# Feed-forward gate and up: the high weights take both parts of the tokens in one pass of 512 columns

## The chip, the cores and the metric

The kernel runs on one core of one Trainium2 chip, in one launch. The metric is the device time of that launch in microseconds (us); three runs of the kernel before gave 3330.14, 3331.45 and 3333.46 us, the median is 3331.45 us. Lower is better.

## What is computed

256 tokens of width 1024 go through two stacks of layers. The first stack has two layers and the second four; every layer is a feed-forward block, a mixer, and a second feed-forward block, so there are 12 feed-forward blocks and six mixers. Everything is float32.

```python
def swiglu(x, w_gate, w_up, w_down):          # [256,1024] -> 2816 -> 1024
    return (silu(x @ w_gate) * (x @ w_up)) @ w_down
# first stack, layer 0: mixer recurrent_block; layer 1: forgetting_attention
h = h + 0.5 * rms_norm(swiglu(rms_norm(h, g1), ...), post1)
h = h + rms_norm(mixer(rms_norm(h, g2)), post2)
h = h + 0.5 * rms_norm(swiglu(rms_norm(h, g3), ...), post3)
# second stack, four layers: gdn, short_conv, nsa, gdn; no norm behind a block
h = h + 0.5 * swiglu(rms_norm(h, g1), ...)
h = h + mixer(rms_norm(h, g2))
h = h + 0.5 * swiglu(rms_norm(h, g3), ...)
```

The gdn mixer (gated delta rule, 8 heads, two chunks of 128 tokens) solves a triangular system for every head and chunk before it can apply its state.

## The kernel before

**Products.** A float32 operand is split into a high part, rounded to the TensorE's fast 32-bit type, and a low part, the rest. A product is then three matmuls into the same sum: high by high, high by low, low by high (`mm3`, lines 159 to 164; the page's L162, L163, L164 are these three). Weights come by DMA as float32 (`raw`), ScalarE makes the high part `whi` (L150, or L154 with a gain), VectorE the low part `wlo` (L151, L155). A unit is 1024 columns of both.

**A feed-forward block** (`ffn`, line 228). The 2816 hidden columns are worked in 11 groups of 256, gate and up together: four units of weights per group. Group 0 has the tokens as the stationary operand (`rows_group`, L266): one token tile of 128 after the other, 24 matmuls of 512 columns each, after which the 128x256 result is activated (`act`, L242: ScalarE's Tanh L244, VectorE's L245 and L246) and transposed back on TensorE (`split_T` of `hid`, L174). Groups 1 to 10 have the weights as the stationary operand (`cols_group`, L278): for 8 chunks of the width, 2 halves of the columns, gate and up, an `mm3` with 256 token columns moving, 96 matmuls in all, into two PSUM banks. Between groups stand the 24 matmuls of the down product of the group before (`down_mm`, L249, weights in a pool of their own), 512 columns moving.

**Between blocks.** `residual` (L322) adds the block's output to the token tile `h[t]` and calls `prep(t)` (L194): mean square on ScalarE (`rstd`, L189), a power on GpSimd (L191), the scaling `xn` on VectorE (L208 or L210), eight transposes on TensorE (L174, `xn`), and the split into `xh` (ScalarE, L175) and `xl` (VectorE, L176). Tile 0 goes first, then tile 1; the next block's first matmuls use tile 0 alone.

**gdn** (L748 on). Heads go in four groups of two. For each group `wcols` (L410) projects q, k and v with the weights stationary (48 matmuls of 256 columns each for q, k, v), VectorE convolves them, and `chunk` (L852) runs the triangular solve: five levels of L892 on TensorE, `Y` on ScalarE (L895), L898 on TensorE, L900 and L903 on VectorE; the two chunks of tokens go side by side.

**Order and buffers.** The program is written block by block; a scheduler then puts each engine's instructions into one fixed order, by priority and by when a buffer can be had. An engine works through its order without overtaking. PSUM has eight banks, taken through `bank(tag)`:

```python
def bank(self, tag, name="ps"):                       # L101
    return self.psum.tile([128, 512], F32, name=name, tag=tag, bufs={"acc": 4}.get(tag, 2))
```

So "acc" (sums of down and output products, and some of gdn's) has four banks, "gu" (gate and up, projections) two and "tr" (transposes, parts of the mixers) two.

Of the kernel before, what the change touches and what calls it, by code (L numbers as in the profile page):

```python
# [8 lines left out]
F32 = mybir.dt.float32  # L9
# [20 lines left out]
def level_masks():  # L30
    """[128, 448]: the blocks (even, odd) of size 1 next to the diagonal; then for b = 2, 4, .. 32 the even
    columns of the mask of the blocks (odd, even) of size b"""
    i = np.arange(128)
    out = np.zeros((128, 448), np.int32)
    for l in range(6):
        blk = i >> l
        low = (blk[:, None] == blk[None, :] + 1) & (blk[:, None] % 2 == 1)
        if l == 0:
            out[:, :128] = low.T
        else:  # L40
            out[:, 64 + 64 * l:128 + 64 * l] = low[:, blk % 2 == 0]
# [23 lines left out]
class Core:  # L65
# [35 lines left out]
    def bank(self, tag, name="ps"):  # L101
        return self.psum.tile([128, 512], F32, name=name, tag=tag, bufs={"acc": 4}.get(tag, 2))
# [7 lines left out]
    def rows_to_cols(self, name, *srcs):  # L110
        """srcs: DRAM [n, w] each -> SBUF [w, sum n] with row r in column r."""
# [47 lines left out]
    def mm3(self, out, l, r, start, stop, skip=False):  # L159
        """out += l.T @ r for operands split in (high, low) parts."""  # L160
# [5 lines left out]
    def split_T(self, src, xh, xl):  # L166
        """transpose the 128-column chunks of src [128, *] into xh/xl [128, chunks, 128]"""
# [26 lines left out]
    def prep(self, t):  # L194
        """transposed split of h[t], normalized (times row_gain, where there is one), into self.x; the
        transposes are left to flush"""
# [15 lines left out]
        self.late = lambda: [self.split_T(xs[n], *[a[:, t, 4 * n:4 * n + 4] for a in x]) for n in range(2)]  # L212
# [3 lines left out]
    def flush(self):  # L216
        """the transposes that prep left, after other work for the tensor engine"""
# [4 lines left out]
    def row(self, src):  # L222
        """a DRAM row of 1024 in all partitions"""
# [4 lines left out]
    def ffn(self, gates, up, down, gain, post, after=None, also=None):  # L228
        """gate / up: DRAM [1024, 2816]; down: [2816, 1024]; gain: [128, 8] columns;
        post: None or DRAM row [1024] of the gain after the block; after: None or such a row for the  # L230
        norm that follows; also: None or what to set up on the way"""
# [5 lines left out]
        xh, xl = self.x  # L237
# [28 lines left out]
        def rows_group(j, t, gu):  # L266
            tok = slice(t * 128, t * 128 + 128)
            p = self.bank("gu")
            for k in range(8):
                wh, wl = gu[k // 2]  # L270
                self.mm3(p, (xh[:, t, k], xl[:, t, k]), (wh[:, k % 2], wl[:, k % 2]), k == 0, k == 7)
            hid = act(p)
# [95 lines left out]
    def project_out_turns(self, xs, w, post):  # L368
        """the same with one token tile after the other"""
# [40 lines left out]
    def wcols(self, outs, wv, gain, c0, n, x=None):  # L410
        """outs[i] [n, 256] = (x @ W[:, c0 + i n : c0 + (i + 1) n]).T; wv: DRAM [128, 8, N]"""
# [3 lines left out]
        xh, xl = x or self.x  # L415
# [3 lines left out]
        for i, out in enumerate(outs):  # L419
            c = slice(i * n, i * n + n)  # L420
            for k in range(8):
                wh, wl = us[k // kg]
                self.mm3(out, (wh[:, k % kg, c], wl[:, k % kg, c]), (xh[:, :, k], xl[:, :, k]), k == 0, k == 7)

    def short_conv(self, w_in, conv, w_out):
        """conv: [128, 24] columns (tap * 8 + block)"""
# [3 lines left out]
        with self.tc.tile_pool(name="sc", bufs=2) as sp:  # L430
            yh = self.xt.tile([128, 8, 256], F32R, name="xh")
            yl = self.xt.tile([128, 8, 256], F32R, name="xl")
# [990 lines left out]
```

## Time and profile before

| | |
|---|---|
| three runs | 3330.14, 3331.45, 3333.46 us |
| span of the profiled execution | 3325.6 us |
| what lies around the span (median less span) | 5.9 us |
| TensorE busy | 3266.9 us, 98% |
| VectorE, ScalarE busy | 2163.9 us (65%), 1781.7 us (54%) |
| DMA | 543.94 MB, 52.6% of 16 engines |

The span runs from the first to the last instruction of the one execution that was profiled; that execution's whole time is not listed apart, so the median of the runs stands in for it. A matmul's row shows how long that one takes from its start to its end; neighbours overlap, so what one more of them costs is the distance of starts. "PE" is TensorE, "PEld" its weight loads, "DVE" VectorE, "ACT" ScalarE, "POOL" GpSimd.

### The profile page before, as it was taken

How to read it: one execution, taken by the hardware profiler on the slowest of the kernel's cores; microseconds unless marked ns; L12 is line 12 of the kernel's file. 1: busy time of each engine (PE TensorE's matmuls, PEld its weight loads, DVE VectorE, ACT ScalarE, POOL GpSimd, SP SyncE). 2: the span in 40 equal slices, each digit the busy share in tenths (PEclk: the TensorE clock that was granted, in tenths of full speed). 3: DMA queues.
4: the chain of work that ended last, by engine and by line, in shares of the span. 5: the costliest groups of instructions: out<-in, count | busy, mean ns of one | idle time of the engine just before them, and what ended most of it. 6: DMA issues, size and time to landing. Idle time of an engine off the chain costs nothing.

```text
span 3325.6 us, 57379 instructions
## 1 busy us (share of the span) xinstructions
PE 3266.9 (98%) x22022; PEld 2950.3 (89%) x22022; DVE 2163.9 (65%) x4039; ACT 1781.7 (54%) x3277; POOL 82.1 (2%) x106
## 2 busy tenths in 40 slices
PE   8999999999999999999999999999999999999999
PEld 8988898988798998989999989899767989989898
DVE  7667766664666657776566575665767566577764
ACT  6557655554555544555555455554566555454653
POOL 0000000000000000000000000000100000000000
PEclk9999999998899999999999999999999999999999
DMA  8643665644465663336656466566515656532463
GB/s 265 193 132 120 216 198 169 186 152 129 145 192 160 208 185 109 102 99 206 189 178 198 145 198 195 158 206 188 143 52 164 186 161 205 179 102 86 133 201 109
DMA packets 422043, 543.94 MB, mean 164 GB/s; under 512 B 36232, under 2 KB 369096, under 8 KB 421768
## 3 DMA queue, kind: packets, MB, share of 16 engines
q1 hardware_dynamic: 421768, 540.27, 52.6%
q8 instruction: 173, 2.83, 0.3%
q14 instruction: 102, 0.84, 0.1%
HBM read 539.12 MB, written 1.05 MB: 162 GB/s over the span
## 4 chain that ended last, share of the span: by engine, by line
PE 88%; DVE 6%; ACT 3%; issue 2%; POOL 1%; DMA 1%; POOLq 0%; SPq 0%; ACTq 0%; DVEq 0%
PE ps L164 26%; PE ps L162 26%; PE ps L163 26%; PE ps L174 1%; PE ps L892 1%; PE ps L898 1%; DVE wlo L155 1%; PE ps L1286 1%; DVE wlo L151 1%; POOL ss L191 1%; PE ps L1310 1%; PE ps L725 1%; ACT sq L189 1%; PE ps L554 1%; ACT whi L150 0%
## 5 line engine op out<-in xcount | busy, mean ns | idle before, releaser
L162 PE MATMUL ps<-xh,whi 128*128 128x256 f32 (+1 forms) x4704 | 1335.0, 284 | 6.7 <-ACT v L839 2.7
L164 PE MATMUL ps<-xh,wlo 128*128 128x256 f32 (+1 forms) x4704 | 1333.7, 284 | 0.0
L163 PE MATMUL ps<-xl,whi 128*128 128x256 f32 (+1 forms) x4704 | 1332.8, 283 | 0.0
L155 DVE SCALAR_TENSOR_TENSOR wlo<-raw,gains,whi 128x512 fp32r<-128x512 f32 (+1 forms) x1024 | 717.1, 735 | 470.8 <-ACT whi L154 457.3
L154 ACT ACTIVATE whi<-raw,gains 128x512 fp32r<-128x512 f32 (+1 forms) x1024 | 676.7, 707 | 560.1 <-issue 265.3
L162 PEld LDWEIGHTS ps<-xh,whi 128*128 128x128 f32 (+1 forms) x4704 | 895.6, 190 | 14.1 <-ACT v L839 3.1
L163 PEld LDWEIGHTS ps<-xl,whi 128*128 128x128 f32 (+1 forms) x4704 | 895.9, 190 | 6.0
L164 PEld LDWEIGHTS ps<-xh,wlo 128*128 128x128 f32 (+1 forms) x4704 | 895.3, 190 | 1.2
L151 DVE TENSOR_TENSOR wlo<-raw,whi 128x1024 fp32r<-128x1024 f32 (+4 forms) x473 | 569.6, 1209 | 270.4 <-ACT whi L150 268.0
L150 ACT CAST whi<-raw 128x1024 fp32r<-128x1024 f32 (+4 forms) x473 | 488.9, 1038 | 298.9 <-DMA raw<-in_ffn_w_down 126.0
L162 PE MATMUL ps<-whi,hh 128*128 128x512 f32 x1056 | 412.7, 391 | 0.0
L163 PE MATMUL ps<-wlo,hh 128*128 128x512 f32 x1056 | 412.6, 391 | 0.0
L164 PE MATMUL ps<-whi,hl 128*128 128x512 f32 x1056 | 411.3, 390 | 0.0
L162 PE MATMUL ps<-whi,xh 128*128 128x512 f32 (+3 forms) x624 | 249.2, 400 | 3.0 <-ACT xh L175 3.0
L164 PE MATMUL ps<-whi,xl 128*128 128x512 f32 (+3 forms) x624 | 245.4, 394 | 2.4 <-DVE xl L176 2.4
L163 PE MATMUL ps<-wlo,xh 128*128 128x512 f32 (+3 forms) x624 | 246.0, 394 | 0.0
L164 PEld LDWEIGHTS ps<-whi,hl 128*128 128x128 f32 x1056 | 197.8, 188 | 43.3 <-DVE hl L293 1.8
L162 PEld LDWEIGHTS ps<-whi,hh 128*128 128x128 f32 x1056 | 198.8, 188 | 38.8 <-ACT hh L292 2.0
L163 PEld LDWEIGHTS ps<-wlo,hh 128*128 128x128 f32 x1056 | 198.3, 188 | 37.5
L244 ACT ACTIVATE hid<-ps 128x256 f32<-128x256 f32 x264 | 99.7, 378 | 132.5 <-PE ps L164 132.2
L245 DVE SCALAR_TENSOR_TENSOR hid<-hid,ps 128x256 f32<-128x256 f32 x264 | 110.2, 418 | 74.4 <-ACT hid L244 74.3
L164 PEld LDWEIGHTS ps<-whi,xl 128*128 128x128 f32 (+2 forms) x624 | 116.7, 187 | 28.1 <-DVE xl L176 6.8
(403 smaller groups left out, 2757.2 us busy)
## 6 DMA issues: line engine op xcount, KB each, us to landing
raw<-in_ffn_w_gate_up SPq DMA_DIRECT2D x704, 256.0 KB
raw<-in_ffn_w_down SPq DMA_DIRECT2D x264, 512.0 KB
raw<-in_ffn_w_gate SPq DMA_DIRECT2D x176, 256.0 KB
raw<-in_ffn_w_up SPq DMA_DIRECT2D x176, 256.0 KB
raw<-in_gdn_w_in SPq DMA_DIRECT2D x64, 512.0 KB
raw<-in_sc_w_in SPq DMA_DIRECT2D x24, 512.0 KB
raw<-in_w_kv SPq DMA_DIRECT2D x16, 512.0 KB
raw<-in_gdn_w_out SPq DMA_DIRECT2D x16, 512.0 KB
```

Of the source, the lines that this page charges most:

```text
L150: nc.scalar.copy(hi, raw)
L151: nc.vector.tensor_sub(lo, raw, f32(hi))
L154: nc.scalar.activation(hi[:, i], raw[:, i], AF.Copy, scale=gain[i])
L155: nc.vector.scalar_tensor_tensor(lo[:, i], raw[:, i], gain[i], f32(hi[:, i]), op0=OP.mult, op1=OP.subtract)
L162: mm(out, l[0], r[0], start=start, stop=False, skip_group_check=skip)
L163: mm(out, l[0], r[1], start=False, stop=False, skip_group_check=skip)
L164: mm(out, l[1], r[0], start=False, stop=stop, skip_group_check=skip)
L174: nc.tensor.transpose(p[:, k], src[:, (i + k) * 128:(i + k + 1) * 128], self.ident)
L189: nc.scalar.activation(sq, p, AF.Square, scale=1 / (32.0 * scale), accum_out=ss[:, i:i + 1])
L191: nc.gpsimd.tensor_tensor(ss[:, 3:4], ss[:, 2:3], self.mhalf[:, :1], op=OP.pow)
L244: nc.scalar.activation(hid, p[:, :256], AF.Tanh, scale=0.5)
L245: nc.vector.scalar_tensor_tensor(hid, hid, 1.0, p[:, :256], op0=OP.add, op1=OP.mult)
```

## The change

In groups 1 to 10 the matmul with the high weights takes the high and the low tokens in one pass: 256 columns of the high part and 256 of the low part, side by side, into one whole bank; a second matmul of 256 columns adds low weights by high tokens to the first half of that bank. The two halves are added afterwards (`joined`): ScalarE copies the second half to SBUF, VectorE adds the first. The loop over the two column halves `i` becomes the outer one, with a bank for gate and one for up in each, four in all where there were two. For this, "gu" and "tr" become one tag of four banks, and the high and low tokens become one tile, in which they alternate by chunk. `hid` has two buffers in place of three.

```diff
     def bank(self, tag, name="ps"):
-        return self.psum.tile([128, 512], F32, name=name, tag=tag, bufs={"acc": 4}.get(tag, 2))
+        return self.psum.tile([128, 512], F32, name=name, tag="acc" if tag == "acc" else "gu", bufs=4)
...
     def by_token(self):
-        return [self.xt.tile([128, 8, 256], F32R, name=n).rearrange("p a b -> p (a b)")
-                .rearrange("p (t k c) -> p t k c", t=2, k=8) for n in ("xh", "xl")]
+        return self.xt.tile([128, 4096], F32R, name="x").rearrange("p (t k l c) -> p t k l c", t=2, k=8, l=2)
...
-        def act(p):
-            hid = dpool.tile([128, 256], F32, name="hid", bufs=3)
-            nc.scalar.activation(hid, p[:, :256], AF.Tanh, scale=0.5)
-            nc.vector.scalar_tensor_tensor(hid, hid, 1.0, p[:, :256], op0=OP.add, op1=OP.mult)
-            nc.vector.scalar_tensor_tensor(hid, hid, 0.5, p[:, 256:], op0=OP.mult, op1=OP.mult)
+        def act(g, u):
+            hid = dpool.tile([128, 256], F32, name="hid", bufs=2)
+            nc.scalar.activation(hid, g, AF.Tanh, scale=0.5)
+            nc.vector.scalar_tensor_tensor(hid, hid, 1.0, g, op0=OP.add, op1=OP.mult)
+            nc.vector.scalar_tensor_tensor(hid, hid, 0.5, u, op0=OP.mult, op1=OP.mult)
             return hid
+        def joined(p):
+            o = dpool.tile([128, 256], F32, name="sum", bufs=3)
+            nc.scalar.copy(o, p[:, 256:])
+            nc.vector.tensor_add(o, o, p[:, :256])
+            return o
...
         def cols_group(j, gu):
-            ps = [self.bank("gu") for _ in range(2)]
-            for k in range(8):
-                wh, wl = gu[k // 2]
-                for i in range(2):
+            hs = []
+            for i in range(2):
+                ps = [self.bank("gu") for _ in range(2)]
+                for k in range(8):
+                    wh, wl = gu[k // 2]
                     for half in range(2):
                         cc = slice(256 * half + 128 * i, 256 * half + 128 * i + 128)
-                        self.mm3(ps[i][:, half * 256:half * 256 + 256], (wh[:, k % 2, cc], wl[:, k % 2, cc]),
-                                 (xh[:, :, k], xl[:, :, k]), k == 0 and half == 0, k == 7, True)
-            hs = []
-            for i in range(2):
-                hid = act(ps[i])
+                        nc.tensor.matmul(ps[half], wh[:, k % 2, cc], x[:, :, k].rearrange("p t l c -> p l t c"),
+                                         start=k == 0, stop=False, skip_group_check=True)
+                        nc.tensor.matmul(ps[half][:, :256], wl[:, k % 2, cc], x[:, :, k, 0],
+                                         start=False, stop=k == 7, skip_group_check=True)
+                hid = act(joined(ps[0]), joined(ps[1]))
                 hh = dpool.tile([128, 256], F32R, name="hh", bufs=4)
```

In the new file the two matmuls are L298 and L300, the copy L256 and the add L257; each of L298 and L300 stands 3840 times in the program (12 blocks, 10 groups, 32). Other users of the tokens only follow the new layout.

The change also moves instructions on TensorE, at places that the diff doesn't show. The first is the passage from one feed-forward block to the next in the second stack. `hh`, `hl` are the hidden columns of the block that ends (its down product), `xn` the normalized tokens to transpose, `whi` and `xh` (or `x`) the first products of the block that begins, with token tile 0. Before:

```order
L164 MATMUL ps<-whi,hl 128x512
L162 MATMUL ps<-whi,xh 128x512
L163 MATMUL ps<-wlo,xh 128x512
L164 MATMUL ps<-whi,xl 128x512
...
L174 MATMUL ps<-ident,xn 128x128 x8
L162 MATMUL ps<-whi,xh 128x512
L163 MATMUL ps<-wlo,xh 128x512
...
L174 MATMUL ps<-ident,hid 128x128 x2
L163 MATMUL ps<-wlo,xh 128x512
```

With the change:

```order
L164 MATMUL ps<-whi,hl 128x512
L174 MATMUL ps<-ident,xn 128x128 x8
L162 MATMUL ps<-whi,x 128x512
L163 MATMUL ps<-wlo,x 128x512
L164 MATMUL ps<-whi,x 128x512
...
L174 MATMUL ps<-ident,hid 128x128 x2
L162 MATMUL ps<-whi,x 128x512
```

Fifteen products of tile 0 stood ahead of the transposes of tile 1 and now stand behind them; and the transposes of `hid` stood seven products into tile 1, and now stand ahead of all of them.

The second place is the triangular solve of gdn, at the first group of heads: L892 and L898 (L900 and L906 in the new file) are two steps of a level, and `xh,whi` with 256 columns are the projections of the group of heads that comes next. Before:

```order
L892 MATMUL ps<-XX,NA 128x64 x4
L162 MATMUL ps<-xh,whi 128x256
L163 MATMUL ps<-xl,whi 128x256
L898 MATMUL ps<-Y,XX 128x64 x4
L164 MATMUL ps<-xh,wlo 128x256
L162 MATMUL ps<-xh,whi 128x256
L163 MATMUL ps<-xl,whi 128x256
L164 MATMUL ps<-xh,wlo 128x256
L892 MATMUL ps<-XX,NA 128x64 x4
```

With the change:

```order
L880 MATMUL ps<-kb,k 128x128 x2
L882 MATMUL ps<-q,k 128x128 x2
L900 MATMUL ps<-XX,NA 128x64 x2
L906 MATMUL ps<-Y,XX 128x64 x2
L900 MATMUL ps<-XX,NA 128x64 x4
L906 MATMUL ps<-Y,XX 128x64 x4
```

Between the first L872 and the first transpose behind the solve stood 106 products of the next group; now there is none, and they stand behind the solve.

## Rows read from the trace of the kernel before

**Rows 1.** The page: span, busy time of the engines, chain that ended last.
```profile
span 3325.6 us, 57379 instructions
...
PE 3266.9 (98%) x22022; PEld 2950.3 (89%) x22022; DVE 2163.9 (65%) x4039; ACT 1781.7 (54%) x3277; POOL 82.1 (2%) x106
...
PE 88%; DVE 6%; ACT 3%; issue 2%; POOL 1%; DMA 1%; POOLq 0%; SPq 0%; ACTq 0%; DVEq 0%
```
**Rows 2.** Timeline, TensorE, one group: start us, us, engine line operation out<-in shapes.
```profile
369.99 0.28 PE L162 MATMUL ps<-xh,whi 128*128 128x256 f32 x1
...
381.50 0.40 PE L162 MATMUL ps<-whi,hh 128*128 128x512 f32 x1
...
386.97 0.28 PE L162 MATMUL ps<-xh,whi 128*128 128x256 f32 x1
```
**Rows 3.** Windows, that group: stretch, length, busy us (count) per engine, clock, DMA.
```profile
369.99:386.97 16.98, 16.98 (x122) 16.02 (x120) 11.27 (x18) 10.91 (x17) 0.00 (x0) 1.00 0.69 217
```
**Rows 4.** Groups by shape: count | busy us, mean ns of one | idle before.
```profile
L245 DVE SCALAR_TENSOR_TENSOR hid<-hid,ps 128x256 f32<-128x256 f32 x264 | 110.2, 418 | 74.4 <-ACT hid L244 74.3
...
L244 ACT ACTIVATE hid<-ps 128x256 f32<-128x256 f32 x264 | 99.7, 378 | 132.5 <-PE ps L164 132.2
```
**Rows 5.** Timeline, TensorE, from a feed-forward block to the next, second stack.
```profile
1672.82 0.39 PE L164 MATMUL ps<-whi,hl 128*128 128x512 f32 x1
1673.05 0.39 PE L162 MATMUL ps<-whi,xh 128*128 128x512 f32 x1
...
1676.26 0.39 PE L164 MATMUL ps<-whi,xl 128*128 128x512 f32 x1
1677.02 1.07 PE L174 MATMUL ps<-ident,xn 128*128 128x128 f32 x8 [0.37 <-DVE xn L208]
```
**Rows 6.** Timeline, VectorE, the same passage.
```profile
1674.37 1.23 DVE L151 TENSOR_TENSOR wlo<-raw,whi 128x1024 fp32r<-128x1024 f32 x1 [0.43 <-ACT whi L150]
...
1676.38 0.88 DVE L208 TENSOR_SCALAR xn<-h,ss 128x512 f32<-128x512 f32 x2 [0.67 <-POOL ss L191]
```
**Rows 7.** Timeline, TensorE, such a passage in the first stack.
```profile
528.08 0.39 PE L164 MATMUL ps<-whi,hl 128*128 128x512 f32 x1
...
537.21 0.39 PE L164 MATMUL ps<-whi,xl 128*128 128x512 f32 x1
538.46 1.06 PE L174 MATMUL ps<-ident,xn 128*128 128x128 f32 x8 [0.86 <-DVE xn L208]
```
**Rows 8.** Timeline, TensorE, first product of tile 1 and transposes of hid.
```profile
1680.00 0.39 PE L162 MATMUL ps<-whi,xh 128*128 128x512 f32 x1
...
1681.64 0.41 PE L174 MATMUL ps<-ident,hid 128*128 128x128 f32 x2
```
**Rows 9.** Windows, gdn's first three solves, from L872 to the transposes behind.
```profile
1309.92:1340.26 30.34, 30.34 (x260) 29.47 (x259) 24.12 (x65) 16.61 (x48) 0.70 (x1) 1.00 0.28 82
1351.06:1384.82 33.76, 33.76 (x256) 31.23 (x257) 26.24 (x67) 17.53 (x50) 0.70 (x1) 1.00 0.39 110
1402.13:1432.32 30.19, 30.08 (x254) 28.89 (x255) 23.38 (x63) 16.82 (x49) 0.69 (x1) 1.00 0.21 68
```
**Rows 10.** Timeline, one level of the first solve, all engines.
```profile
1321.11 1.00 PE L892 MATMUL ps<-XX,NA 128*128 128x64 f32 x8
...
1321.75 0.27 ACT L895 COPY Y<-ps 128x128 f32<-128x128 f32 x1 [1.91 <-PE ps L892]
...
1322.23 1.00 PE L898 MATMUL ps<-Y,XX 128*128 128x64 f32 x8
...
1322.83 0.75 DVE L900 COPY_PREDICATED XX<-masks,ps 128x128 f32<-128x128 uint8 x2 [0.72 <-PE ps L898]
...
1323.61 0.67 PE L892 MATMUL ps<-XX,NA 128*128 128x64 f32 x5
```
**Rows 11.** Windows, behind the first block's end: clock in the last column but two.
```profile
201.10:204.10 3.00, 1.64 (x10) 0.84 (x8) 1.75 (x5) 1.71 (x5) 2.44 (x5) 1.00 0.00 0
204.10:211.20 7.10, 7.04 (x27) 5.98 (x27) 5.50 (x9) 1.92 (x5) 4.76 (x8) 0.76 0.34 58
```

More of the change, by code (lines that the diff above doesn't have):

```diff
@@ L178, in by_token, with by_chunk @@
     def by_token(self):
-        return [self.xt.tile([128, 8, 256], F32R, name=n).rearrange("p a b -> p (a b)")
-                .rearrange("p (t k c) -> p t k c", t=2, k=8) for n in ("xh", "xl")]
+        return self.xt.tile([128, 4096], F32R, name="x").rearrange("p (t k l c) -> p t k l c", t=2, k=8, l=2)
+    def by_chunk(self):
+        y = self.xt.tile([128, 4096], F32R, name="x").rearrange("p (l k c) -> p l k c", l=2, k=8)
+        return y[:, 0], y[:, 1]
     def rstd(self, parts, scale=1.0):
@@ L211, in prep @@
             xs.append(xn)
-        self.late = lambda: [self.split_T(xs[n], *[a[:, t, 4 * n:4 * n + 4] for a in x]) for n in range(2)]
+        self.late = lambda: [self.split_T(xs[n], *[x[:, t, 4 * n:4 * n + 4, l] for l in range(2)]) for n in range(2)]
         if t == 1:
@@ L236, in ffn @@
         dv = down.rearrange("(k p) n -> p k n", p=128)
-        xh, xl = self.x
+        x = self.x
         acc = [[None, None], [None, None]]
@@ L270, in rows_group @@
                 wh, wl = gu[k // 2]
-                self.mm3(p, (xh[:, t, k], xl[:, t, k]), (wh[:, k % 2], wl[:, k % 2]), k == 0, k == 7)
-            hid = act(p)
+                self.mm3(p, (x[:, t, k, 0], x[:, t, k, 1]), (wh[:, k % 2], wl[:, k % 2]), k == 0, k == 7)
+            hid = act(p[:, :256], p[:, 256:])
             hh = dpool.tile([128, 2, 128], F32R, name="hh", bufs=4)
@@ L414, in wcols @@
         kg = 1024 // w
-        xh, xl = x or self.x
+        x = self.x if x is None else x
         us = [self.weights([(0, wv[:, k0:min(8, k0 + kg), c0:c0 + w])],
@@ L422, in wcols @@
                 wh, wl = us[k // kg]
-                self.mm3(out, (wh[:, k % kg, c], wl[:, k % kg, c]), (xh[:, :, k], xl[:, :, k]), k == 0, k == 7)
+                self.mm3(out, (wh[:, k % kg, c], wl[:, k % kg, c]), (x[:, :, k, 0], x[:, :, k, 1]), k == 0, k == 7)
     def short_conv(self, w_in, conv, w_out):
@@ L430, in short_conv @@
         with self.tc.tile_pool(name="sc", bufs=2) as sp:
-            yh = self.xt.tile([128, 8, 256], F32R, name="xh")
-            yl = self.xt.tile([128, 8, 256], F32R, name="xl")
+            yh, yl = self.by_chunk()
             bT = sp.tile([128, 4, 256], F32, name="bT", bufs=1)
@@ L516, in recurrent @@
         with self.tc.tile_pool(name="rg", bufs=2) as sp:
-            yh = [self.xt.tile([128, 8, 256], F32R, name="xh"), sp.tile([112, 4, 256], F32R, name="yh", bufs=1)]
-            yl = [self.xt.tile([128, 8, 256], F32R, name="xl"), sp.tile([112, 4, 256], F32R, name="yl", bufs=1)]
+            yh, yl = [[a, sp.tile([112, 4, 256], F32R, name=n, bufs=1)] for a, n in zip(self.by_chunk(), ("yh", "yl"))]
             ys = [(yh[c // 8][:112, c % 8], yl[c // 8][:112, c % 8]) for c in range(12)]
@@ L624, in project @@
         kg = min(8, 1024 // w)
-        xh, xl = x or self.x
+        x = self.x if x is None else x
         us = [self.weights([(i * w0, wv[:, k0:k0 + kg, c:c + w0]) for i, c in enumerate(cs)],
@@ L631, in project @@
             p = self.bank(tag)[:, :w]
-            tok = slice(t * 128, t * 128 + 128)
             for k in range(8):
                 wh, wl = us[k // kg]
-                self.mm3(p, (xh[:, t, k], xl[:, t, k]), (wh[:, k % kg], wl[:, k % kg]), k == 0, k == 7)
+                self.mm3(p, (x[:, t, k, 0], x[:, t, k, 1]), (wh[:, k % kg], wl[:, k % kg]), k == 0, k == 7)
             yield t, p
@@ L640, in project_few @@
         nc = self.nc
-        xh, xl = x or self.x
+        x = self.x if x is None else x
         wh, wl = self.weights([(0, wv[:, :, c0:c0 + w])], None if gain is None else [gain[:, k:k + 1] for k in range(8)], (8, w))
@@ L644, in project_few @@
         for k in range(8):
-            self.mm3(p, (wh[:, k], wl[:, k]), (xh[:, :, k], xl[:, :, k]), k == 0, k == 7)
+            self.mm3(p, (wh[:, k], wl[:, k]), (x[:, :, k, 0], x[:, :, k, 1]), k == 0, k == 7)
         y = pool.tile([w, 256], F32, name="few", bufs=1)
@@ L705, in forgetting @@
             qT = sp.tile([128, 8, 256], F32, name="qT", bufs=1)
-            yh = self.xt.tile([128, 8, 256], F32R, name="xh")
-            yl = self.xt.tile([128, 8, 256], F32R, name="xl")
+            yh, yl = self.by_chunk()
             for i in range(0, 8, 2):
@@ L798, in gdn @@
             nc.scalar.activation(eg, gc[:, 1], AF.Exp)
-            yh = self.xt.tile([128, 8, 256], F32R, name="xh")
-            yl = self.xt.tile([128, 8, 256], F32R, name="xl")
+            yh, yl = self.by_chunk()
             def inputs(gr):
@@ L1182, in nsa @@
             vcd = one("vcd", [128, 8, 2, 64])
-            bhl = [self.xt.tile([128, 8, 256], F32R, name=n) for n in ("xh", "xl")]
+            bhl = self.by_chunk()
             def compress(i):
@@ L1245, in nsa @@
             caught_up()
-            yh = self.xt.tile([128, 8, 256], F32R, name="xh")
-            yl = self.xt.tile([128, 8, 256], F32R, name="xl")
+            yh, yl = self.by_chunk()
             pcT = one("pcT", [128, 2, 256])
```

## The prediction

> **What bounds the kernel now.** I read the page first. TensorE is busy for 98% of the span, and 88% of the chain that ended last is its matmuls [rows 1]: an engine that never rests, so a change pays where it takes work from TensorE and costs where it makes TensorE wait. Next the timeline of one feed-forward group, to price a matmul by the distance of starts and not by its row. The 96 matmuls of gate and up start from 369.99 to 381.50, 11.51 us, or 119.9 ns each; the 24 of the down product take from there to 386.97, 5.47 us, or 227.9 ns each [rows 2]. So 512 columns cost less than twice 256: about 12 ns per matmul don't depend on its columns. In the same group VectorE has 11.27 us to do in 16.98 and ScalarE 10.91 [rows 3]: room on both.
>
> That is the inside of a group. Then I looked at the places where the order of TensorE changes, because 98% busy means that the order of before has something to do at every wait. At the passage between blocks the last down product starts at 1672.82, tile 0 of the next block fills the time from 1673.05 to 1676.26, and tile 1's transposes come at 1677.02, when `xn` is ready after an idle 0.37 us [rows 5]. The wait of almost 4 us for the residual, the mean square, the power and the scaling is there today; it is covered. In gdn the solve waits for ScalarE and VectorE at every step and is covered by projections: three stretches of 30 to 34 us with TensorE busy throughout [rows 9].
>
> **The change, part by part.**
>
> *1. One matmul fewer in three.* Three of 256 cost 359.7 ns; one of 512 and one of 256 cost 347.8: 11.9 ns less [rows 2]. The pattern of 512 and 256 by turns is not in the trace; where 512 follows 256 and the other way round (381.50, 386.97) the starts show nothing extra. 3840 times 11.9 ns is **-45.7 us**. At the least it is nothing, at the most the 12 ns of overhead and a little more, 50 us. The Trainium skill (TensorE: Matmul & The Clock Gate, section on the back-to-back issue gap) gives a warm gap of columns divided by 2.4 GHz plus 2.5 ns, which makes 327.5 ns of the three and 325.0 of the two, and a gain of 9.6 us; the measured distances lie 11 and 12 ns above that rule, and the sum goes by them.
>
> *2. Copies and adds.* Per group four copies of 128x256 on ScalarE, priced as its Tanh at 378 ns, and four adds on VectorE at 418 [rows 4]: 10.91 becomes 12.4 and 11.27 becomes 12.9 us of a group that now takes 16.6 [rows 3]. TensorE stays the bound and these cost nothing inside. Behind the last group of a block there is no next group: copy, add, Tanh, two products, cast and difference are some 3 us of such rows, and with the weight splits queued between them about 4.7, against 19 down products that still stand ahead, 4.3 us. I take 0.4 us for each of 12 blocks, **+5 us**, between nothing and 12.
>
> *3. The passages.* The new order puts all transposes of tile 1 ahead of the first product of tile 0, at every passage between a block and a mixer or the next block: 18 of them, counting the start. Transposes and gate/up sums now draw on the same four banks, and TensorE cannot overtake. What covered the wait comes after it. At the passage shown 15 matmuls move behind it, 15 x 228 ns = 3.4 us [rows 5]. By the two orders, there move 24 matmuls at six passages (the first stack and the entry to the second), 18 and 16 at two, 15 at three, 13 at four, 12 at two, 5 at the start: 304, at 228 ns 69 us. One in the first stack, in full: products of tile 0 until 537.21, an idle 0.86 us, transposes at 538.46 [rows 7]; there the wait is longer than its cover, so all 5.5 us are lost. I take off 3 us, because the first product behind the transposes no longer waits for their copies: **+66 us**. The wait itself may shrink, since tile 0's activation and some weight splits now come later: one such split of 1.23 us stands in the way in the passage shown [rows 6]. Up to 0.6 us each, so the lower end is 55; the upper is 69.
>
> *4. Transposes of `hid`.* At 1680.00 tile 1's first product starts, and the transposes of tile 0's `hid` run at 1681.64, seven products later [rows 8]. They now stand ahead of all products of tile 1, and TensorE waits those 1.64 us out: 12 blocks, **+20 us**. For tile 1 the new order has eleven down products in between, 2.5 us: covered, nothing.
>
> *5. gdn.* Each gdn has four solves. By the orders 123, 85 and 118 projections stood inside the first three up to the last transpose behind them; six are left, so 320 x 119.9 ns = 38.4 us leave the cover and come afterwards. Against that an uncovered solve is faster. One level takes 2.50 us [rows 10]; without projections the first `Y` is ready at 1322.02, L898 can follow and L900 after that, and I read 2.0 us off the same rows. Five levels give back 2.5 us, the next group's convolution on VectorE, no longer between the steps, some 2 more: 4.5 in each of three, 13.5. Each group then waits about 1 us more for its own convolution. 38.4 - 13.5 + 3 = 28 us, twice: **+56 us**. Bounds: a solve of 30.34 us holds 106 projections, 12.7 us, so TensorE's own part is 17.6 [rows 9]. If nothing but that were left, a gdn would lose only the waits and the products of the output projection that now stand in one block, some 6 us, 12 for both; if no solve got faster, 41, or 83.
>
> *6. The other mixers* lose cover too (in nsa the compressed blocks' transposes and the rotations, elsewhere less). I count five or six waits of 1 to 3 us: **+10 us**, between 0 and 25.
>
> *7. The clock.* Behind the first block TensorE had little but transposes from 201.10 to 204.10, and in the 7.10 us that follow its granted clock is 0.76 on average [rows 11]: part at 1.2 GHz, the rest at 2.4, a loss of 0.24 x 7.1 = 1.7 us. Waits of that length, covered today, become bare at 18 passages. I take seven such stretches, **+12 us**, between 2 and 31.
>
> **The sum.** -45.7 + 5 + 66 + 20 + 56 + 10 + 12 = +123 us on the span of 3325.6 [rows 1], 3449; with the 5.9 us around it, **3454 us** against a median of 3331.45, 3.7% slower. The gain is real and of its full size, and what moves costs nearly four times as much.
>
> **The rivals.**
>
> *Faster.* The waits shrink when nothing stands beside them. Much of a covered wait may be queueing: VectorE is busy for 24 of the 30 us of a solve [rows 9], largely with the convolution of the next heads, and the same at the passages. If the 18 passages exposed 1 us each in place of 3.7 and the solves fell to TensorE's own 17.6 us: -46 + 5 + 18 + 10 + 4 = -9, 3322 us. It decides once terms 3 to 7 together stay under some 40 us. Against it: in [rows 5] TensorE is idle ahead of the transposes although it had 15 products to do, and in [rows 6] `xn` waits for the power, not for VectorE. 7%.
>
> *Half of it hides.* The solves alone come near TensorE's own time, the passages go as summed: -46 + 5 + 60 + 18 + 16 + 5 + 4 = +62, 3394 us. For it: L892 and L898 show 2.0 us of a 2.5 us level as TensorE's own [rows 10]. 21%.
>
> *The pass gives nothing.* The overhead goes with the columns, so that 512 with a change of weights every time cost twice 256; or its four pieces of 128 columns stream worse than two. Then term 1 falls to 0 to 10 us: 3490 to 3500 us. By the skill's rule above it would be 3490. Against it: the 227.9 ns already hold a change of weights each [rows 2]. 8%.
>
> *More at the low clock.* The long bare waits of the first stack and gdn's bare solves pull the clock down beyond seven stretches, say 30 of them at 1.7 us: +51 in place of +12, about 3493 us. For it: [rows 11] fell after 3 us. Against it: TensorE stays at work in the solves. 12%.
>
> **How the numbers follow.** The forecast, with its terms within a third of what I take, has 49% and covers some 3415 to 3490. With the last two rivals upwards (0.08 + 0.12) and the hidden half downwards (0.21) I reach 3375 to 3545; the lower end is the sum with every term at its low end, -46 + 0 + 55 + 18 + 12 + 0 + 2 = +41, the upper with high ends, -46 + 12 + 69 + 20 + 83 + 25 + 31 = +194, 3525, and a little for both rivals at once. A difference of 0.2% (7 us) is about what a measurement of this kernel can tell from no change. Faster by more: 0.07, the first rival less its part near zero and a little from elsewhere; the same: 0.03; slower: 0.90.
>
> **What would show it.** Right: L298 and L300 start 228 and 120 ns apart inside a group, 32 pairs in 11.1 us; some 4 us (second stack) to 10 us (first stack) without a product between the last down product and tile 0's first; 1.6 us ahead of the transposes of `hid`, in each block; gdn's solves at 25 to 28 us with nothing of `x` between L900 and L906; TensorE's busy share well under 98%. Wrong: pairs at 360 ns (term 1), solves near 18 us (term 5), tile 1's `xn` ready within 2 us of the last down product (term 3), clock rows under 1.00 over tens of us (term 7).

## The result and the profile after

The changed kernel takes **3611.4 us** (median of 4 runs, 3605.5 to 3613.2) where the kernel before took 3331.6 in the same comparison: the ratio is 1.083, with an interval of 1.081 to 1.085. The forecast was slower, 3454 us; the loss is 280 us and not 123, and lies above the range.

The page of the kernel after, with the lines that answer to [rows 1], and the clock in 40 slices of the span:

```profile
span 3608.0 us, 50616 instructions
...
PE 3357.1 (93%) x18182; PEld 2865.1 (79%) x18182; DVE 2343.8 (65%) x4519; ACT 1934.9 (54%) x3759; POOL 83.8 (2%) x106
...
PEclk9999999997999997789999999999899999967999
...
PE 86%; DVE 7%; ACT 3%; issue 2%; POOL 1%; DMA 1%; SPq 0%; POOLq 0%; ACTq 0%; DVEq 0%
```

There are 3840 matmuls fewer, and yet TensorE is busy for 90 us more (3357.1 against 3266.9). Inside a group the change takes time off TensorE (below), so its work elsewhere must take longer, and the line of the clock says why: the mean granted clock is 0.939, where before it was 0.990. A share at 1.2 GHz of 2 x (1 - 0.939) is 440 us of the span; before it was 67. The first seven is the forgetting attention (812 to 902 us), where the kernel before has a low clock too; the other sevens and the six stand in the two gdn stages.

Inside a group the change does what it was forecast to do. The timeline of one group, TensorE, as [rows 2], and its window, as [rows 3]:

```profile
424.24 0.39 PE L298 MATMUL ps<-x,whi 128*128 128x512 f32 x1
...
435.34 0.40 PE L162 MATMUL ps<-whi,hh 128*128 128x512 f32 x1
...
440.83 0.39 PE L298 MATMUL ps<-x,whi 128*128 128x512 f32 x1
```
```profile
424.24:440.83 16.59, 16.59 (x90) 14.21 (x88) 11.64 (x21) 10.01 (x19) 0.00 (x0) 1.00 0.59 187
```

Gate and up run from 424.24 to 435.34: 32 pairs in 11.10 us, 347 ns a pair, forecast 347.8. The group takes 16.59 us in place of 16.98, 0.39 less, 47 us over 120 groups. Copies and adds stand on ScalarE and VectorE beside it, with 10.01 and 11.64 us of 16.59.

At a passage (second stack, and behind it one of the first) the last down product, tile 1's transposes, tile 0's first product and the transposes of `hid` answer to [rows 5], [rows 7] and [rows 8]:

```profile
1813.66 0.39 PE L164 MATMUL ps<-whi,hl 128*128 128x512 f32 x1
1817.85 1.94 PE L174 MATMUL ps<-ident,xn 128*128 128x128 f32 x8 [3.80 <-DVE xn L212]
1819.44 0.78 PE L162 MATMUL ps<-whi,x 128*128 128x512 f32 x1
...
1828.36 0.41 PE L174 MATMUL ps<-ident,hid 128*128 128x128 f32 x2 [1.48 <-DVE hid L250]
```
```profile
545.60 0.39 PE L164 MATMUL ps<-whi,hl 128*128 128x512 f32 x1
547.53 1.06 PE L174 MATMUL ps<-ident,xn 128*128 128x128 f32 x8 [1.54 <-DVE xn L212]
555.90 1.94 PE L174 MATMUL ps<-ident,xn 128*128 128x128 f32 x8 [7.30 <-DVE xn L212]
```

The waits are bare, as forecast: 3.80 us in the second stack, 7.30 in the first, 1.48 ahead of `hid`. New is what follows: eight transposes take 1.94 us where they took 1.07 [rows 5]. They run at half clock, and so do the first eight of tile 0's 24 products (0.43 us apart to 1823.00, 0.23 behind). The windows of the 24 products of tile 0 and of the same 24 of tile 1 right behind:

```profile
1819.44:1826.88 7.44, 7.44 (x26) 5.65 (x24) 1.39 (x2) 0.71 (x2) 0.00 (x0) 0.76 0.25 74
1828.52:1834.07 5.55, 5.55 (x26) 4.60 (x26) 3.55 (x6) 4.21 (x7) 0.00 (x0) 1.00 0.09 18
```

The same work, 7.44 us at a granted clock of 0.76 and 5.55 at 1.00. In gdn it goes further. The windows of the first three solves, as [rows 9] (where they took 30.34, 33.76 and 30.19 us, all at 1.00), and a level of the first, all engines, as [rows 10]:

```profile
1364.80:1400.80 36.00, 31.01 (x154) 29.09 (x152) 16.10 (x51) 9.97 (x36) 0.70 (x1) 0.57 0.09 28
1433.42:1480.62 47.20, 40.63 (x202) 35.66 (x201) 23.36 (x59) 15.18 (x42) 0.70 (x1) 0.71 0.23 66
1512.37:1547.09 34.72, 29.96 (x154) 28.34 (x153) 15.69 (x49) 9.97 (x36) 0.69 (x1) 0.61 0.08 28
```
```profile
1376.48 1.91 PE L900 MATMUL ps<-XX,NA 128*128 128x64 f32 x8
...
1377.63 0.27 ACT L903 COPY Y<-ps 128x128 f32<-128x128 f32 x1 [2.29 <-PE ps L900]
...
1378.18 1.92 PE L906 MATMUL ps<-Y,XX 128*128 128x64 f32 x8
...
1379.89 0.63 PE L900 MATMUL ps<-XX,NA 128*128 128x64 f32 x2
```

The first solve has 154 matmuls in place of 260 and takes 36.0 us in place of 30.3. Its levels show no gap on TensorE at all: eight products of 64 columns take 1.91 us, where before they took 1.00, and a level takes 3.41 us (1376.48 to 1379.89), where before it took 2.50. The solve was to become a chain of waits; at 1.2 GHz it is a chain of TensorE.

Where TensorE waits is shown by the view of waits of the kernel after (engine, line, what it waited for: us in all, times, longest):

```profile
PE ps L174 <- DVE xn L212: 67.8, 22, 8.5
PE ps L174 <- DVE xn L214: 32.5, 12, 6.7
PE ps L174 <- DVE on L980: 23.3, 22, 3.0
PE ps L900 <- DVE XX L894: 22.5, 12, 2.8
PE ps L823 <- ACT th L857: 21.8, 6, 3.6
PE ps L174 <- DVE hid L250: 12.3, 8, 2.0
PE ps L797 <- DVE g L794: 12.1, 2, 6.1
```

In the kernel before, the same view has 23.3 us for `xn` (15.2 and 8.1), and of the other five only `on`, with 1.5 us, among its eleven longest. The four of gdn (`on`, `XX`, `th`, `g`) make 80 us.

### The profile page after: what moved, and what is told of

Same layout as the page of the kernel before. It is cut to its first block, busy times and chain, and to the rows that moved or that the text cites. A ratio compares the mean times of both kernels' runs of the same rounds, so it can differ in the third digit from the quotient of the medians.

```text
span 3608.0 us, 50616 instructions
## 1 busy us (share of the span) xinstructions
PE 3357.1 (93%) x18182; PEld 2865.1 (79%) x18182; DVE 2343.8 (65%) x4519; ACT 1934.9 (54%) x3759; POOL 83.8 (2%) x106
## 4 chain that ended last, share of the span: by engine, by line
PE 86%; DVE 7%; ACT 3%; issue 2%; POOL 1%; DMA 1%; SPq 0%; POOLq 0%; ACTq 0%; DVEq 0%
PE ps L298 24%; PE ps L162 13%; PE ps L163 12%; PE ps L164 12%; PE ps L300 12%; PE ps L174 2%; PE ps L906 1%; PE ps L900 1%; DVE wlo L151 1%; ACT sq L193 1%; POOL ss L195 1%; PE ps L1317 1%; DVE wlo L155 1%; PE ps L1293 1%; PE ps L734 1%
## 5 line engine op out<-in xcount | busy, mean ns | idle before, releaser
L298 PE MATMUL ps<-x,whi 128*128 128x512 f32 x3840 | 1338.9, 394 | 0.0
L300 PE MATMUL ps<-x,wlo 128*128 128x256 f32 x3840 | 1065.0, 277 | 0.0
L298 PEld LDWEIGHTS ps<-x,whi 128*128 128x128 f32 x3840 | 720.1, 188 | 166.2
L300 PEld LDWEIGHTS ps<-x,wlo 128*128 128x128 f32 x3840 | 721.2, 188 | 3.9
L256 ACT COPY sum<-ps 128x256 f32<-128x256 f32 x480 | 169.5, 367 | 396.6 <-PE ps L300 392.5
L257 DVE TENSOR_TENSOR sum<-sum,ps 128x256 f32<-128x256 f32 x480 | 187.7, 417 | 296.6 <-ACT sum L256 296.6
L162 PE MATMUL ps<-whi,x 128*128 128x512 f32 (+3 forms) x624 | 259.5, 416 | 1.0 <-ACT x L175 0.9
L162 PE MATMUL ps<-x,whi 128*128 128x256 f32 (+2 forms) x864 | 259.3, 300 | 0.0
L163 PE MATMUL ps<-x,whi 128*128 128x256 f32 (+2 forms) x864 | 256.0, 296 | 0.0
L164 PE MATMUL ps<-x,wlo 128*128 128x256 f32 (+2 forms) x864 | 255.8, 296 | 0.0
L163 PE MATMUL ps<-wlo,x 128*128 128x512 f32 (+3 forms) x624 | 251.9, 404 | 0.3 <-DVE wlo L155 0.3
L164 PE MATMUL ps<-whi,x 128*128 128x512 f32 (+3 forms) x624 | 250.3, 401 | 0.0
```

The lines of the kernel that those rows point to most:

```text
L162: mm(out, l[0], r[0], start=start, stop=False, skip_group_check=skip)
L163: mm(out, l[0], r[1], start=False, stop=False, skip_group_check=skip)
L164: mm(out, l[1], r[0], start=False, stop=stop, skip_group_check=skip)
L256: nc.scalar.copy(o, p[:, 256:])
L257: nc.vector.tensor_add(o, o, p[:, :256])
L298: nc.tensor.matmul(ps[half], wh[:, k % 2, cc], x[:, :, k].rearrange("p t l c -> p l t c"), start=k == 0, stop=False, skip_group_check=True)
```

## The experiments

All experiments are named by their labels. Two theories stood at the start. A: the line that lets sums and transposes draw on one set of four banks moves TensorE's order, the order makes the loss, and the clock is a large part of it. B: something else in the change (copies, adds, one tile for the tokens) makes it.

### The line on the banks alone, and the change without it

`e1_one_tag` is the kernel before with this line alone:

```diff
-        return self.psum.tile([128, 512], F32, name=name, tag=tag, bufs={"acc": 4}.get(tag, 2))
+        return self.psum.tile([128, 512], F32, name=name, tag="acc" if tag == "acc" else "gu", bufs=4)
```

> The kernel before with one line changed: the sums of gate and up and all transposes draw on one set of four banks (as in the change). Nothing else of the change is in it: three matmuls of 256 columns as before, tokens in two tiles, no copies and adds. Theory A (the shared set of banks alone moves the order, and the order makes the loss): TensorE's order is that of the change at every passage, transposes of hid and in gdn, so the run shows the loss without the gain: the 280 us of the change plus the 50 us that its groups gained (12 blocks x 10 groups x 0.394 us = 47 us), some 3655 us (3635 to 3675), with some 45 stretches at 1.2 GHz as in the change, over 400 us in all. Rival B (the copies and adds of halves, the tokens in one tile or the longer end of a block make the loss): within 60 us of the kernel before, 3331 to 3390 us, with few stretches at 1.2 GHz.

Measured: 3648.1 us, 1.095 of the kernel before (1.093 to 1.096), mean clock 0.940. `e3_turns` is the change with that line undone and with one more:

```diff
-                ps = [self.bank("gu") for _ in range(2)]
+                ps = [self.bank(("gu", "tr")[i]) for _ in range(2)]
```

> The change with two lines altered: banks are in two sets of two again (one for the sums, one for transposes), and the pass of 512 columns takes its two banks from the one set for the first 128 columns of a group and from the other for the second. Gain, copies, adds and the one tile of tokens stay. Theory A (order): TensorE's order in gdn and at the passages is that of the kernel before again; gain of the groups 47 us, copies and adds at the ends of 12 blocks +5 us: 3285 to 3295 us, clock as before (about 70 us at 1.2 GHz). Rival B (the pass itself, its copies and adds or the one tile of tokens make the loss): slower than 3331 us, 3400 to 3600 us.

Measured: **3288.2 us, 0.988 of the kernel before (0.985 to 0.991)**, mean clock 0.990. It beats both kernels: by 45 us the one before (3332.8 in this comparison), by 323 the change. The page of `e3_turns`, then windows of its first solve and of one group:

```profile
span 3285.3 us, 50585 instructions
...
PE 3222.8 (98%) x18182; PEld 2735.6 (83%) x18182; DVE 2322.4 (71%) x4519; ACT 1917.8 (58%) x3757; POOL 83.8 (3%) x106
```
```profile
1294.93:1325.27 30.34, 30.34 (x261) 29.47 (x260) 23.99 (x65) 16.62 (x49) 0.70 (x1) 1.00 0.26 82
371.02:387.61 16.59, 16.59 (x89) 14.22 (x88) 13.46 (x24) 9.70 (x18) 0.00 (x0) 1.00 0.80 248
```

So the loss comes with one line (315 us here, where the change has 323 over `e3_turns`) and goes with it; theory B falls. The group has the 16.59 us of the change, and the solve has the 30.34 us of the kernel before, with 261 matmuls where that had 260. That banks of one set are handed out in the order of the program, and that this keeps later work from being moved ahead, is how I read it; `e4_gdn_only` and `e5_not_gdn` below, which impose that order with two sets, fit it.

`e3_turns` is also the measure of the rest. It runs the same 18182 matmuls as the change, and the difference of the two spans, 322.7 us, splits into 134.3 us that TensorE is busy longer (3357.1 - 3222.8) and 188.4 us that it is idle longer.

`e2_two_tags` undoes the line alone, so that the pass has two banks only.

> The change with the line on the banks alone undone: sums draw on two banks, transposes on two. The pass of 512 columns then has both its banks taken by the first 128 columns of a group, and the second 128 must wait until copy and add have read them. Theory A (banks are what the pass needs; the order is that of the kernel before): a copy of 0.37 and an add of 0.42 us, twice, stand between the halves of a group; where down products lie between them it costs nothing, where not 0.5 to 1 us for each of 120 groups: 3288 to 3400 us, in every case well under the change. Rival (the order moves back only with two more banks for the pass): near the change, 3550 us or more.

Measured: 3341.3 us, 1.002 (1.000 to 1.004). Its view of waits starts with a line that `e3_turns` doesn't have:

```profile
PE ps L298 <- DVE sum L257: 23.9, 24, 2.0
```

The order is back, but the gain is gone: the first product of the pass waits for the add of the half before. The pass needs its second pair of banks, and `e3_turns` takes it where the transposes leave theirs unused.

### gdn and the rest apart

`e4_gdn_only` and `e5_not_gdn` are `e3_turns` with banks taken by turns in the order of the program, in gdn alone or everywhere else; `e0_all` does it everywhere. The lines that all three share:

```diff
+        if self.pooled and tag != "acc":
+            self.turn += 1
+            tag = ("gu", "tr")[self.turn % 2]
...
```

> As e3_turns, but within gdn alone the sums and transposes take the four banks by turns in the order of the program, so that gdn has the order of the change (no projections inside its solves) and the passages and the other mixers have that of the kernel before. Theory A (most of what the forecast missed lies in gdn, where bare solves run at 1.2 GHz): each gdn stage 85 to 100 us longer than in e3_turns, with some 120 us at 1.2 GHz in each: e3_turns + 170 to 200 us, 3455 to 3490 us. By the forecast's own term for gdn: e3_turns + 56 us (12 to 83), 3340 to 3370 us. Rival C (the miss lies in the passages and in the other mixers): under e3_turns + 60 us as well.

Measured: 3454.0 us, 166 over `e3_turns`, mean clock 0.957. The windows of both gdn stages, from the last sum of the block ahead to the first of the block behind, in `e3_turns`, in `e4_gdn_only` and in the change:

```profile
1240.40:1481.11 240.71, 234.17 (x1683) 210.20 (x1681) 182.11 (x454) 125.72 (x302) 18.00 (x20) 1.00 0.35 107
2868.99:3109.80 240.81, 234.23 (x1682) 210.22 (x1681) 182.18 (x454) 125.97 (x302) 18.00 (x20) 1.00 0.35 104
```
```profile
1241.27:1566.49 325.22, 285.14 (x1683) 256.13 (x1681) 187.04 (x454) 129.09 (x302) 16.29 (x20) 0.82 0.26 79
2952.15:3276.41 324.26, 284.60 (x1682) 255.34 (x1681) 187.02 (x454) 129.23 (x302) 16.29 (x20) 0.83 0.26 77
```
```profile
1294.83:1643.31 348.48, 290.50 (x1696) 264.07 (x1694) 191.16 (x459) 131.78 (x305) 16.29 (x20) 0.81 0.25 76
3086.91:3435.29 348.38, 290.55 (x1695) 264.12 (x1694) 190.99 (x459) 131.85 (x305) 16.29 (x20) 0.81 0.25 74
```

The two stages lose 168 us in `e4_gdn_only` and 215 in the change, of a loss of 323. Theory A's range, 170 to 200 us, began 4 us too high; the forecast's own term for gdn, 56 us, is far off.

> The counterpart of e4_gdn_only: gdn keeps the order of the kernel before (two sets of two banks), everything else takes the four banks by turns, in the order of the program, as in the change. If the loss is the sum of its places, this costs what is left of it: 3611 - 3288 - 166 = 157 us over e3_turns, 3445 us (3430 to 3460), of which the forecast's terms for passages, transposes of hid, other mixers and clock make 66 + 20 + 10 + 12 = 108 us. If gdn and the rest share a cost (a clock that falls in one and is paid in the other), the sum of both is off by more than 20 us.

> All stages take the two sets of two banks by turns in the order of the program (gdn as in e4_gdn_only, the rest as in e5_not_gdn). This tells what e4 and e5 leave open: they add 166 and 111 us to e3_turns, together 277, where the change has 323. If the places add and the missing 47 us are those in which taking turns is not the same as one set of four (seven products of tile 1 stand ahead of the transposes of hid, a passage of the first stack differs), this run is at 3288 + 277 = 3565 us (3555 to 3578). If gdn and the rest make each other worse, it is near the change, 3600 us or more.

Measured: `e5_not_gdn` 3398.8 us, 111 over `e3_turns` and not 157; `e0_all` 3535.7 us and not 3565. Both expectations fail, for two reasons. The first is a double count: the passages into and out of gdn were moved in `e4_gdn_only` and in `e5_not_gdn` alike, and the gdn stages of the latter are 27 us longer (253.9 and 254.5 us, from 1278.06 and 2966.86, in place of 240.7 and 240.8). Counted once, 166 + 111 - 27 = 250 us, and `e0_all` has 247. So the places add. The second is that turns are milder than one set of four by 76 us, of which 50 lie in the two gdn stages (323 us each in `e0_all`, 348 in the change). The 157 us took the whole loss of the change for that of turns: 157 - 76 + 27 = 108, and `e5_not_gdn` has 111. The order of `e0_all` has seven products of tile 1 ahead of the transposes of `hid`; what else makes the 76 us I did not take apart.

### The clock, in gdn and at the passages

A wait and a low clock come together, so the question was what the clock itself costs. The experiments put matmuls that nobody reads into the waits of the change. Without them TensorE's order in `e8_fill_passages` is that of the change, matmul by matmul; in `e7_fill2` and `e9_fill_both` 818 of the 18182 stand at another place (400 in `e6_fill`), all of them in gdn. `e6_fill` was the first try.

```diff
...
+            def fill(gr, t, n):
+                if gr < 3 and t == 1 and n:
+                    p = self.bank("acc")[:, :256]
+                    for _ in range(n):
+                        nc.tensor.matmul(p, fx[:, 0, 0, 0], fx[:, :, 0, 0], start=True, stop=True)
...
```

> The change itself with 516 more matmuls of 256 columns, whose results nobody reads, put between the steps of the first three solves of each gdn (86 per solve, behind the steps at which TensorE waits). Theory A (the clock falls because TensorE waits, and at 1.2 GHz the steps themselves take longer): with something to do in the waits the clock stays at 2.4 GHz, a level takes 2.3 to 2.6 us in place of 3.41, each of the six solves is 6 to 12 us shorter although it has 10 us more to do, and projections behind the solves run at 2.4 GHz as well: 40 to 100 us less than the change, 3510 to 3570 us. Rival D (the steps wait for ScalarE and VectorE, the low clock costs little): as long as the change, or up to 516 x 0.12 = 62 us longer, 3611 to 3673 us.

Measured: 3616.5 us, no gain. The trace decides neither way: the time at 1.2 GHz in the gdn stages fell from 259 to 154 us (their mean clock rose), but ten fillers in a level stand in TensorE's way: in the first solve such a level takes 5.55 us at 1.2 GHz (1380.78 to 1386.33) and 2.98 at 2.4 (to 1389.31). What the clock gave, the fillers took. `e7_fill2` puts fewer into the levels and more into the long waits that the view of waits lists (48 ahead of L797, 28 ahead of L823, 22 behind L882, 22 ahead of `on`).

> The change with 890 matmuls of 256 columns, whose results nobody reads, in gdn alone, placed by where e6_fill and the change showed TensorE idle: 48 in the wait of 6.07 us ahead of the first sums over tokens, 28 in each wait of 3.63 us ahead of L823, 22 in the wait of 2.85 us behind L882, 22 in the wait of 2.97 us inside the transposes of the result, and only 6 in a level (e6_fill had 10), with 9 in the first level where the second tile is not there yet. At 0.12 us those in the long waits are no longer than the waits. Theory A (the low clock is itself the cost: at 1.2 GHz a level is 3.41 us of TensorE without a gap): the time at 1.2 GHz in the two gdn stages falls from 259 us to under 100, a solve from 42.3 to 33 to 38 us, and the run is 40 to 110 us faster than the change: 3500 to 3570 us. Rival D (the solves are bound by their chain, whatever the clock): no faster than e6_fill, 3611 us or more.

Measured: 3559.7 us, 51.7 less than the change, though it runs 890 matmuls more. The windows of its first solve and of both gdn stages:

```profile
1360.89:1392.00 31.11, 29.66 (x248) 28.25 (x249) 17.46 (x55) 10.87 (x40) 0.70 (x1) 1.00 0.09 28
```
```profile
1293.17:1616.63 323.46, 299.44 (x2141) 273.34 (x2139) 190.65 (x459) 131.95 (x305) 16.80 (x20) 0.97 0.28 82
3061.17:3384.36 323.19, 298.46 (x2141) 272.10 (x2139) 190.65 (x459) 132.03 (x305) 16.79 (x20) 0.98 0.27 80
```

The solve falls from 36.00 to 31.11 us and each stage by 25 us; the clock is a cost and not a companion. What a bare solve takes at 2.4 GHz it doesn't show, since fillers stand in the chain: a level with six of them takes 2.49 us (1372.99 to 1375.48), all of it TensorE. A level without any stands in the change itself, in the second solve, right behind the products of the gate. Timeline of TensorE and window:

```profile
1463.17 1.00 PE L900 MATMUL ps<-XX,NA 128*128 128x64 f32 x8
1464.17 1.10 PE L906 MATMUL ps<-Y,XX 128*128 128x64 f32 x8
1465.22 0.66 PE L900 MATMUL ps<-XX,NA 128*128 128x64 f32 x4
```
```profile
1463.17:1465.22 2.05, 2.05 (x17) 1.83 (x15) 2.05 (x4) 1.71 (x4) 0.00 (x0) 1.00 0.93 275
```

It takes 2.05 us, where a level took 2.50 among projections and takes 3.41 at 1.2 GHz. From the last product of the solve to the first transpose `e7_fill2` has 3.18 us with 22 fillers (1388.81 to 1391.99), where the fourth solve of the change, at 1.00, has 1.22 (1610.68 to 1611.90). So a bare solve at 2.4 GHz would be at some 28 us; that is an estimate, 31.1 less 2.0 and less three times 0.44.

`e8_fill_passages` leaves gdn alone and fills the waits ahead of tile 1's transposes, with 56 matmuls or 28.

```diff
...
+            if self.old is not None:
+                p = self.bank("gu")[:, :256]
+                for _ in range(n_fill):
+                    nc.tensor.matmul(p, self.old[:, 0, 0, 0], self.old[:, :, 0, 0], start=True, stop=True)
             self.flush()
...
```

> The change with 644 matmuls of 256 columns, whose results nobody reads, at 17 passages, ahead of the transposes of tile 1: 56 (6.7 us) where a gain follows the block (waits of 7.3 us), 28 (3.4 us) elsewhere (waits of 3.8 us). gdn is left as in the change. Theory A (the clock falls in these waits, and the 24 products behind the transposes then take 7.4 us in place of 5.55): the stretches at 1.2 GHz at the ends of blocks go, and each passage is 1.5 to 3 us shorter: 25 to 50 us less than the change, 3560 to 3586 us. Rival (the wait alone is the cost, the clock gives nothing back): 3605 to 3620 us, and if the extra matmuls don't lie inside the waits up to 77 us more.

Measured: 3571.3 us, 40 less than the change. The passage that answers to the one at 1817.85 above, timeline of TensorE:

```profile
1785.39 3.51 PE L222 MATMUL ps<-x 128*128 128x256 f32 x28
...
1789.34 1.06 PE L174 MATMUL ps<-ident,xn 128*128 128x128 f32 x8 [0.44 <-DVE xn L213]
...
1797.35 0.30 PE L174 MATMUL ps<-ident,hid 128*128 128x128 f32 x1 [1.48 <-DVE hid L255]
```

The fillers lie inside the wait (0.44 us of it is left), the transposes take 1.06 us again, and from them to those of `hid` it is 8.01 us in place of 10.51: 2.5 us for this passage. Not all of the 40 us is of this kind: 18 lie in the stage of the forgetting attention (188.9 us, 206.8 in the change), where a stretch of 44 us at 1.2 GHz that the kernel before has too is gone as well. The other 22 are the passages: every other stage differs by less than 4 us.

> The extra matmuls of e7_fill2 and of e8_fill_passages together in the change (1534, results read by nobody). If the clock's price is paid in each place by itself, the two savings add: 51.7 + 40.1 us off 3611.4, some 3520 us (3505 to 3535), and what is left over e3_turns (3288), some 230 us, is waiting and moved work at 2.4 GHz. If the stretches at 1.2 GHz share a cause (a budget that is used up elsewhere), the sum is off by more than 20 us.

Measured for both together: 3529.2 us, 82 less than the change at a mean clock of 0.983, where 92 would be the sum of the two. The missing 10 us are those of the forgetting attention, whose stage is back at 209.2 us in the profiled execution; of the four runs two are near 3520 and two near 3539. So the prices add to within 10 us, and no budget is shared. The windows of its gdn stages:

```profile
1288.05:1609.34 321.29, 305.08 (x2197) 279.29 (x2195) 190.34 (x459) 131.56 (x305) 16.77 (x20) 0.98 0.28 82
3045.62:3362.86 317.24, 300.55 (x2196) 275.28 (x2195) 190.40 (x459) 131.60 (x305) 16.76 (x20) 0.99 0.27 82
```

So the low clock that the change brings costs 73 us at least (the spans, 3608.0 - 3535.5, with the attention's stretch in both), in medians 82. The fillers that stand in the solves hide some 3.3 us more in each of six, 20 us, by the estimate above. At most it is the 134 us that the same matmuls are busy longer, and part of those is waiting too, since a product that is followed by nothing shows its whole length. The Trainium skill (TensorE: Matmul & The Clock Gate, Terms) puts the penalty at the throttled time times the share of pulses taken away: half of the 373 us more at 1.2 GHz would be 186 us, an estimate from that rule. The runs stay under it; as I read them, because in part of that time TensorE waited for other engines.

## Why the prediction was wrong in size

All sums here are made on the spans of the profiled executions: forecast 3449 us, found 3608, a miss of 159.

**Terms 1 and 2, right.** -45.7 and +5 make -41 us; `e3_turns`, which has them and the old order, has 3285.3 - 3325.6 = -40. The rival in which the pass gives nothing is out: 347 ns a pair, not 360.

**Terms 3, 4 and 6, right but for the clock.** The waits at the passages are the forecast ones, 3.80 and 7.30 us, and 1.48 ahead of `hid`. Of these terms (66 + 20 + 10) some 18 us lie in the gdn stages, 9 in each, and 78 outside. With the clock held (`e9_fill_both`, mean clock 0.983 where `e3_turns` has 0.990) the stages outside gdn lose 93 us over `e3_turns`: 3535.5 - 3285.3 = 250, less the 157 of the two gdn stages (321.3 and 317.2 us). That is 15 too little in the sum. I put most of it down to the other mixers, whose waits I had only counted; no run takes them apart.

**Term 7, the clock, is the first step that failed.** I took seven stretches, +12 us, and set 31 as the highest. I had the price from [rows 11] and applied it to the passages alone; the rival of thirty stretches was set aside with "TensorE stays at work in the solves". It does, but with products of 64 columns at 1.2 GHz, some 30 us in each of six solves, and at that clock they are the chain. Found: 73 us at least, 61 over the term. The sign that the forecast named for this, clock rows under 1.00 over tens of us, is in the first solve: 0.57 over 36 us. That rival was right in its mechanism and named gdn's bare solves, but its 51 us were too few because it priced each stretch at the 1.7 us of a passage.

**Term 5, gdn, is the second.** With the clock held, the two stages lose 157 us over `e3_turns`; I had 56 and the 18 for their passages, 83 less. The projections do leave the cover (none is left in the first and the third solve). "Each group then waits about 1 us more for its own convolution" was wrong: the view of waits has 3.6 us ahead of L823, six times, and 6.1 ahead of L797, twice, 34 us in all and not 6, 28 of the 83. From L880 to the first transpose of the result the four solves of `e7_fill2` take 31.1, 44.6, 31.1 and 33.1 us, where the kernel before has 30.3, 33.8, 30.2 and 30.6. That is 15 us more in each gdn and not 13.5 less. Of it 11 us, 22 for both, is the block of 48 products of the gate that now stands as one in the second solve (48 x 0.228), where the kernel before has 32 of them among the steps; the forecast has no term for it. Some 20 us for both are the fillers, by the estimate above. The remaining 13 I did not take apart.

What was right in this term is the level: 2.0 us were read off the rows, and 2.05 stand in the change where the clock is 1.00. But the forecast has its solves at 25 to 28 us, and they take 36.0, 47.2 (with the gate's block) and 34.7, as at 1.2 GHz a level is 3.41. So the saving that the rivals "faster" and "half of it hides" also built on is there at 2.4 GHz, as far as the one level shows it, and the clock takes it and more. No run has a whole bare solve at 2.4 GHz without fillers.

61 + 83 + 15 us is the miss. How it divides between the two steps hangs on the fillers: if their 20 us are left out of gdn, 81 go to the clock and 63 to gdn.

## What to carry to other kernels

Before a tag of on-chip banks is widened or merged, compare the order of the instructions in stages that the edit never touches: here one line moved 320 products of each gdn out of the waits that they covered, in a mixer that the edit doesn't name, and the gain was to be had without it when the second pair of banks was borrowed where it lay idle. A wait that becomes bare on TensorE has two prices, its length and the slower work behind it, and the second is dearest where that work is a chain of small products. A covered chain can be shorter when it is bare (2.05 us a level in place of 2.50), and a low clock can take back more than that (3.41): price it at both levels of the clock.

## What the runs showed of the hardware

The clock can fall and stay low while TensorE has no gap. In the forgetting attention of the kernel before, the windows ahead of it, at its start and behind:

```profile
765.00:795.00 30.00, 30.00 (x252) 30.00 (x251) 13.35 (x11) 13.27 (x16) 0.00 (x0) 1.00 0.58 179
796.00:802.00 6.00, 6.00 (x45) 4.68 (x43) 3.44 (x8) 3.74 (x9) 0.00 (x0) 1.00 0.58 180
803.00:846.00 43.00, 43.00 (x172) 24.15 (x171) 15.23 (x58) 15.84 (x57) 0.00 (x0) 0.50 0.03 12
```

TensorE is busy for all of the 79 us shown, first with projections and then with the small products and transposes of the attention; from 802.4 on, 44 us run at 1.2 GHz. In `e2_two_tags` this stretch stayed at 1.00. There the whole stage is 21 us shorter: 166.80 us (718.13 to 884.93) in place of 187.88 (710.20 to 898.08 in the kernel before). In gdn of the change the clock stays low in the same way: from 1373.04 to 1386.72 TensorE is at work for all of the 13.68 us, at 0.50. So a busy TensorE, as the view of engines shows it, is no sign that the clock stays; only the clock's own column is. What in those products makes the difference was not tried.

Runs of one kernel differ by the clock too: seven runs of the kernel before in the last comparison go from 3317.9 us at a mean clock of 0.995 to 3344.6 at 0.985, 27 us for 67 more at 1.2 GHz.
